# A gate table in DRAM: one-hot products replaced by indirect accumulating transfers, and 104 blocks spilled instead of 64

## The chip, the cores and the metric

One NeuronCore of one Trainium2 chip. TensorE is PE in the profile (its weight loads PEld), VectorE DVE, ScalarE ACT, GpSimd POOL, SyncE SP. SP issues the plain DMAs, POOL the indirect ones; both kinds run on the core's 16 DMA engines. The metric is the device time of one launch in microseconds (us), as the median of several runs.

## The reference, cut to what matters

One decoder layer on 512 tokens of width 1024: three kinds of attention beside each other, an output projection, then a retrieval network (PEER). Only the last is touched by the change:

```
qry = h @ w_q                                   # 8 heads x 256 per token
s1, s2 = scores of either half against 128 sub-keys
v1, i1 = top_k(s1, 16); v2, i2 = top_k(s2, 16)
top_s, pos = top_k(all v1[a] + v2[b], 16)       # of 256 pairs
expert = i1 * 128 + i2 at pos                   # 16 of 16384 experts per head
gate = softmax(top_s)
a = h . u[expert]; w = gelu(a) * gate
out = sum over the 128 (head, slot) of w * v[expert]
```

u and v are tables of 16384 rows of 1024 floats (64 MB each).

## The kernel before, in words

The tokens stand in four chunks of 128. After the attention (`attention`, L272) and the output projection (`mix_out`, L355) the retrieval is done in two ways.

Chunk 0 (`GC`) gathers its rows: for each of its 128 slots POOL gathers one u row per token by an indirect DMA (`gather`, L473), DVE multiplies it with the token's vector and sums (L482). When all 128 are there, the v rows are gathered too, scaled and added (L490 to L493), half of them on DVE, half by ACT and POOL.

Chunks 1 to 3 (`DC`, 384 tokens) go through the whole tables. The experts are cut into 128 blocks by their second index. For a block b, `u_parts` (L514) loads 512 KB of u and splits it into a high half (ACT) and a low half (DVE or POOL), and `a_block` (L521) forms gelu(u h) for 128 experts x 384 tokens with 24 PE matmuls of 384 columns. `w_block` (L628) multiplies this with the block's slice of a gate table (L645), which has a token's gate where it chose the expert and zero elsewhere, splits the product and a 512 KB block of v, and adds the product to eight accumulated sums in PSUM (18 PE matmuls of 512 columns, six banks). These banks are held to the end, so this second product starts only when the banks are free of other uses.

So the first `NSP` = 64 blocks are spilled: phase A (L603 to L610) forms their gelu(u h) and stores them in DRAM (`ad`), one step of the gathers after each block (`tc.issue_after` puts the step's instructions behind the last low split on that split's engine). The second stage (L655 on) forms the 64 others in place, loads the spilled ones again, and does the v products of all 128; what remains of the gathers goes beside it.

The queries, scores and top-16 of all heads are formed in a loop over four groups of two heads (L536 to L576): chunk 0's routing (`route`, L413: pair sums, top-16 of 50 candidates, look-up of the expert by compare, product and sum, L440 to L443, softmax of the gates) stands inside it, that of the other chunks after it. Then the gate table is made per chunk: expert and gate are transposed; for four tokens at a time DVE compares both indices with 0 to 127 (L591, L592), DVE or ACT multiplies the gate in (L595, L597), one PE product per token gives the 128 x 128 table of that token (L600), ACT copies it out (L601), and twelve stores of 2 MB put it into DRAM (L602). The second stage reads it back in 384 pieces of 64 KB (L637).

The order in which each engine issues its instructions is fixed when the program is built: a planner plays the program through with its own table of costs, and of what is ready takes what stands earlier in the program. Each engine then works its queue off in that order; POOL's holds its arithmetic and its indirect DMAs.

Of the kernel before, what the change touches and what calls it, by code (L numbers as in the profile page):

```python
# [22 lines left out]
P = 128  # L23
S = 512
NT = S // P
D = 1024
# [4 lines left out]
NK = 128  # L31
PH = 8
TK = 16
NSLOT = PH * TK
EPS = 1e-6
GC = 0
DC = [c for c in range(NT) if c != GC]
NSP = 64
GT = 32
LEAD = 2  # L40
NB = 4
BANKS = dict(s=4, t=2, o=2)
CYC = "stosstos"
WB = 4
SCB = 4
UL = "GGGG"
EM = 4
OGD = "AV"
GR = 1.0
TD = P * len(DC)  # L50
GROUPS = ((0, 1, 2), (3, 4, 5), (6, 7))
# [5 lines left out]
def layer_kernel(ctx, tc, x, xT, memT, mem, w_in, w_kv, w_out, w_q, cols, qk_gain, g_bc, subT, bias_tab,  # L57
# [4 lines left out]
    def tile_pool(**kw):  # L62
        return tc.tile_pool(reuse_waits="tile", **kw)
# [2 lines left out]
    dram = ctx.enter_context(tc.tile_pool(name="dram", bufs=1, space=DRAM))  # L66
    st = ctx.enter_context(tile_pool(name="st", bufs=8))
    xd = [dram.tile([P, D], F32, name=f"xd{c}") for c in range(NT)]
    gd = [[dram.tile([P, NK, GT], F32, name=f"gd{c}_{q}") for q in range(P // GT)] for c in range(len(DC))]
    ad = [dram.tile([P, TD], F32, name=f"ad{b}") for b in range(NSP)]  # L70

    ident = top.tile([P, P], F32, name="ident")
# [196 lines left out]
    tv = [[peer.tile([P, PH, TK], F32, name=f"tv{c}{i}") for i in range(2)] for c in range(NT)]  # L269
    ti = [[peer.tile([P, PH, TK], U32, name=f"ti{c}{i}") for i in range(2)] for c in range(NT)]  # L270

    def attention(chunks, yT, rg, name):  # L272
        base, W = chunks[0] * P, len(chunks) * P
        n_evac = 0
        last = chunks[-1]
        with tile_pool(name=f"sm{name}", bufs=2) as sm:
# [5 lines left out]
                              bias_tab[3 * i + 3:3 * i + 6, :, S - TW:S].rearrange("h p u -> p h u"))  # L282
            ones = sm.tile([P, P], F32, name="ones", bufs=1)
            V.memset(ones, 1.0)
            sqs = []
            for pair in range(8):
                o_ps = bank("o")
# [122 lines left out]
        for q in range(len(src)):  # L410
            V.max_index(idx[q][:, 8:16], vals[q][:, 8:16], rest[q])

    def route(c, dst=None, q0=0, nq=PH):  # L413
# [6 lines left out]
        V.tensor_scalar(tf[0], ti[c][0][:, qs, :], float(NK), None, ALU.mult)  # L420
        V.tensor_copy(tf[1], ti[c][1][:, qs, :])
        cv = tile_([nq, NCAND], "cv")
        ci = tile_([nq, NCAND], "ci")
        for d_, (one, two) in ((cv, [t[:, qs, :] for t in tv[c]]), (ci, tf)):
            off = 0
            for a, n in CAND:
                V.tensor_add(d_[:, :, off:off + n], two[:, :, 0:n], one[:, :, a:a + 1].to_broadcast([P, nq, n]))
                off += n
            V.tensor_add(d_[:, :, off:off + 8], one[:, :, 8:16], two[:, :, 0:1].to_broadcast([P, nq, 8]))
        wv = tile_([nq, TK], "wv")  # L430
        wi = tile_([nq, TK], "wi", U32)
        for q in range(0, nq, 4):
            some = range(q, min(q + 4, nq))
            top16(NCAND, [cv[:, r, :] for r in some], [wv[:, r, :] for r in some], [wi[:, r, :] for r in some], rp, "w")
        wf = tile_([nq, TK], "wf")
        V.tensor_copy(wf, wi)
        ex = tile_([nq, TK], "ex")
        for q in range(nq):
            eq = rp.tile([P, TK, NCAND], F32, tag="eq", name="eq", bufs=2)
            V.tensor_tensor(eq, wf[:, q, :, None].to_broadcast([P, TK, NCAND]),  # L440
                            iota[:, None, 0:NCAND].to_broadcast([P, TK, NCAND]), ALU.is_equal)
            (V if q < EM and nq == PH else G).tensor_mul(eq, eq, ci[:, q, None, :].to_broadcast([P, TK, NCAND]))
            V.tensor_reduce(ex[:, q, :], eq, AX.X, ALU.add)  # L443
        wm = tile_([nq], "wm")
        V.tensor_copy(wm, wv[:, :, 0])
# [7 lines left out]
        ef = ex.rearrange("p h k -> p (h k)")  # L453
        if c == GC:
            sl = slice(q0 * TK, (q0 + nq) * TK)
# [3 lines left out]
        gt = tile_([NSLOT], "gt")  # L459
        V.tensor_mul(gt.rearrange("p (h k) -> p h k", k=TK), pe, rb)  # L460
        ei = tile_([NSLOT], "ei", I32)
        V.tensor_copy(ei, ef)
        e12 = tile_([2, NSLOT], "e12", I32)
        V.tensor_scalar(e12[:, 0, :], ei, 7, None, ALU.arith_shift_right)
        V.tensor_scalar(e12[:, 1, :], ei, NK - 1, None, ALU.bitwise_and)
        f12 = tile_([2, NSLOT], "f12")
        V.tensor_copy(f12, e12)
        tp = quarters(bank("o"))[:, 0:3, :]
        for i, s_ in enumerate((f12[:, 0, :], f12[:, 1, :], gt)):
            T.transpose(tp[:, i, :], s_, ident)  # L470
        A.activation(dst, tp, AF.Copy)

    def gather(table, s_):  # L473
        row = gr.tile([P, D], F32, tag="row", name="row")
# [55 lines left out]
    with tile_pool(name="qa", bufs=1) as qa, tile_pool(name="qp", bufs=2) as qp:  # L530
        mix_out([GC] + DC, yT, rg, hT, "l")
        for t in ga:
            G.memset(t, 0.0)
        rp = ctx.enter_context(tile_pool(name="rp", bufs=1, side="right"))
        sub = qa.tile([P, 2 * PH, NK], F32, name="sub", bufs=1)
        for n in range(4):  # L536
            for k2 in range(KD // 2):
# [24 lines left out]
            for i in range(4):  # L562
# [8 lines left out]
                for j in range(len(DC)):  # L571
# [5 lines left out]
    with tile_pool(name="oh", bufs=2) as oh:  # L577
        loaded = 0
        steps = gather_all()
        for ci_, c in enumerate(DC):  # L580
            iT = oh.tile([P, 3, P], F32, tag="iT", name="iT")
            route(c, iT)
            for q in range(P // GT):
                stage = oh.tile([P, NK, GT], F32, tag="stage", name="stage")
                for t4 in range(0, GT, 4):
                    t0 = q * GT + t4
                    bc = lambda a: a[:, t0:t0 + 4, None].to_broadcast([P, 4, NK])
                    ib = iota[:, None, :].to_broadcast([P, 4, NK])
                    o1 = oh.tile([P, 4, NK], F32, tag="o1", name="o1", bufs=3)
                    o2 = oh.tile([P, 4, NK], F32, tag="o2", name="o2", bufs=3)  # L590
                    V.tensor_tensor(o1, bc(iT[:, 0, :]), ib, ALU.is_equal)  # L591
                    V.tensor_tensor(o2, bc(iT[:, 1, :]), ib, ALU.is_equal)  # L592
                    og = oh.tile([P, 4, NK], F32, tag="og", name="og", bufs=3)
                    if OGD[t4 // 4 % len(OGD)] == "V":
                        V.tensor_mul(og, o2, bc(iT[:, 2, :]))  # L595
                    for j in range(0 if OGD[t4 // 4 % len(OGD)] == "V" else 4):
                        A.activation(og[:, j, :], o2[:, j, :], AF.Copy, scale=iT[:, 2, t0 + j:t0 + j + 1])  # L597
                    gp = quarters(bank("s"))
                    for j in range(4):
                        T.matmul(gp[:, j, :], o1[:, j, :], og[:, j, :], start=True, stop=True)  # L600
                    A.activation(stage[:, :, t4:t4 + 4].rearrange("p e t -> p t e"), gp, AF.Copy)  # L601
                DMA.dma_start(gd[ci_][q], stage)  # L602
        for b in range(NSP):  # L603
            while loaded < min(b + 4, NSP):
                u_parts(loaded, loaded % 4, dict(G=G, V=V)[UL[loaded % len(UL)]])
                loaded += 1
            DMA.dma_start(ad[b], a_block(b))
            for s_ in range(int(GR * b), int(GR * (b + 1))):
                with tc.issue_after(last_lo[-1].ins):
                    next(steps)  # L610

    vs_src = v.rearrange("(a b) w -> b a w", b=NK)
    with tile_pool(name="vb", bufs=2) as vb:
# [14 lines left out]
        def w_block(n, b, ag):  # L628
# [2 lines left out]
                DMA.dma_start(ag, ad[b])  # L631
            g0 = b // NB * NB
            if g0 not in gtiles:
                gt = vb.tile([P, NB, len(DC), P], F32, tag="gt", name="gt")
                for ci_ in range(len(DC)):
                    for q in range(P // GT):
                        DMA.dma_start(gt[:, :, ci_, q * GT:(q + 1) * GT], gd[ci_][q][:, g0:g0 + NB, :])  # L637
# [7 lines left out]
            V.tensor_mul(w.rearrange("p (c t) -> p c t", t=P), ag.rearrange("p (c t) -> p c t", t=P),  # L645
                         gt[:, b % NB, :, :])
# [93 lines left out]
```

## Time and profile before

| | before |
|---|---|
| median of 3 runs | 1754.92 us (1753.0 to 1755.09) |
| span of the profiled execution | 1749.3 us; no time of its own stands beside it |
| PE busy | 1592.6 us (91%) |
| DVE busy | 1442.9 us (82%) |
| POOL busy | 968.3 us (55%) |
| ACT busy | 787.2 us (45%) |
| moved by DMA | 390.08 MB, mean 223 GB/s |
| mean granted clock of TensorE | 0.963 |

The span is from the first to the last instruction; the run's time is a little longer. Busy shares are averages over stages with different limits, so the rows below look at stretches. In a row of an instruction group, "idle" is the time in which the engine waited just before such an instruction, and for whom.

### The profile page before, as it was taken

The numbers are of one execution on the slowest core, as the hardware profiler recorded it, in microseconds if no ns is written. First come the engines' busy times: TensorE is split into PE (matmuls) and PEld (weight loads), VectorE is DVE, ScalarE is ACT, GpSimd is POOL, SyncE is SP. The second block draws the span as 40 slices with busy tenths as digits, with TensorE's granted clock in tenths as the row PEclk, the third lists the DMA queues.
The fourth block names the chain that finished last, engine by engine and source line by source line (L and its number), as shares of the span: only waits on it lengthen the run. The fifth ranks groups of instructions, "written<-read, shape, count | busy, mean of one in ns | idle before, by whom it ended". The sixth has DMA issues, their size and how long they took to land.

```text
span 1749.3 us, 23459 instructions
## 1 busy us (share of the span) xinstructions
PE 1592.6 (91%) x8045; PEld 1397.1 (80%) x8045; DVE 1442.9 (82%) x2552; ACT 787.2 (45%) x1287; POOL 968.3 (55%) x531
## 2 busy tenths in 40 slices
PE   7999989997686878878999999999999999899997
PEld 6886667997686777778998888888888888788885
DVE  6556745899999999979956877877889978889896
ACT  6345633332332555667843333334444443444442
POOL 4220013363776675734465544456778867788774
PEclk9999999998888989889999999999999999999998
DMA  8302034132566566557699999998999999898894
GB/s 322 106 25 103 1 121 144 49 125 90 181 212 198 182 218 216 176 222 280 231 315 325 279 318 288 315 286 279 291 287 278 317 290 275 255 309 276 288 277 171
DMA packets 317463, 390.08 MB, mean 223 GB/s; under 512 B 214944, under 2 KB 240544, under 8 KB 314656
## 3 DMA queue, kind: packets, MB, share of 16 engines
q1 hardware_dynamic: 280480, 254.36, 46.0%
q0 software_dynamic: 36864, 134.23, 21.6%
q8 instruction: 63, 1.03, 0.2%
q14 instruction: 56, 0.46, 0.1%
HBM read 346.57 MB, written 41.94 MB: 222 GB/s over the span
## 4 chain that ended last, share of the span: by engine, by line
PE 49%; DVE 36%; issue 5%; DMA 5%; ACT 2%; SPq 2%; POOL 2%; DVEq 0%; ACTq 0%; POOLq 0%
PE s L96 7%; PE s L97 7%; PE s L95 6%; PE t L95 5%; PE t L97 5%; PE t L96 5%; DVE row L482 5%; DVE o L591 5%; DVE o L592 4%; PE o L96 3%; PE o L97 3%; PE o L95 3%; DVE eq L440 2%; PE o L330 2%; DVE og L595 2%
## 5 line engine op out<-in xcount | busy, mean ns | idle before, releaser
L87 POOL TENSOR_TENSOR yT<-flat,yT 128x1024 fp32r<-128x1024 f32 x128 | 346.6, 2709 | 216.4 <-ACT yT L86 208.7
L95 PE MATMUL t<-hT,yT 128*128 128x384 f32 x1024 | 351.4, 343 | 26.1 <-ACT ag L527 26.1
L97 PE MATMUL t<-hT,yT 128*128 128x384 f32 x1024 | 351.4, 343 | 2.4 <-POOL yT L87 2.4
L96 PE MATMUL t<-hT,yT 128*128 128x384 f32 x1024 | 350.3, 342 | 0.0
L87 DVE TENSOR_TENSOR yT<-vr,yT 128x1024 fp32r<-128x1024 f32 x128 | 209.5, 1637 | 54.7 <-ACT yT L86 51.5
L475 POOL DMA_INDIRECT row<-u,exp_g x128 | 161.7, 1263 | 124.0 <-DVE row L482 88.3
L95 PEld LDWEIGHTS t<-hT,yT 128*128 128x128 f32 x1024 | 197.0, 192 | 32.5 <-ACT ag L527 27.3
L96 PE MATMUL s<-yT,ws 128*128 128x512 f32 x512 | 206.7, 405 | 11.1 <-DVE yT L87 10.8
L482 DVE SCALAR_TENSOR_TENSOR row<-row,hg 128x1024 f32<-128x1024 f32 x128 | 189.2, 1482 | 24.0 <-DMA row<-u,exp_g 24.0
L97 PE MATMUL s<-yT,ws 128*128 128x512 f32 x512 | 201.4, 402 | 4.2 <-DVE ws L87 4.2
L475 POOL DMA_INDIRECT row<-v,exp_g x128 | 156.1, 1219 | 84.9 <-DVE ga L493 49.6
L86 ACT ACTIVATE ws<-w 128x384 fp32r<-128x384 f32 x128 | 67.1, 524 | 299.4 <-DVE w L645 118.7
L97 PEld LDWEIGHTS t<-hT,yT 128*128 128x128 f32 x1024 | 196.8, 192 | 5.7 <-POOL yT L87 3.0
L96 PEld LDWEIGHTS t<-hT,yT 128*128 128x128 f32 x1024 | 196.8, 192 | 4.5
L86 ACT ACTIVATE yT<-flat 128x1024 fp32r<-128x1024 f32 x128 | 135.4, 1058 | 144.2 <-issue 53.6
L491 POOL TENSOR_TENSOR ga<-ga,row 128x1024 f32<-128x1024 f32 x64 | 164.1, 2564 | 26.1 <-ACT row L490 25.4
L95 PE MATMUL s<-yT,ws 128*128 128x512 f32 x512 | 165.1, 399 | 7.8 <-ACT ws L86 7.8
L86 ACT ACTIVATE yT<-vr 128x1024 fp32r<-128x1024 f32 x128 | 134.2, 1048 | 57.4 <-DMA vr<-v 44.0
L600 PE MATMUL s<-og,o 128*128 128x128 f32 x768 | 109.7, 296 | 54.8 <-DVE og L595 38.4
L600 PEld LDWEIGHTS s<-og,o 128*128 128x128 f32 x768 | 103.1, 208 | 63.4 <-issue 39.6
L87 DVE TENSOR_TENSOR ws<-w,ws 128x384 fp32r<-128x384 f32 x128 | 119.8, 937 | 41.0 <-ACT ws L86 36.2
L493 DVE SCALAR_TENSOR_TENSOR ga<-row,gw,ga 128x1024 f32<-128x1024 f32 x64 | 143.2, 2238 | 6.6 <-DMA row<-v,exp_g 6.4
(268 smaller groups left out, 3249.2 us busy)
## 6 DMA issues: line engine op xcount, KB each, us to landing
flat<-uT SPq DMA_DIRECT2D x128, 512.0 KB
vr<-v SPq DMA_DIRECT2D x128, 512.0 KB
gd<-stage SPq DMA_DIRECT2D x12, 2048.0 KB
gt<-gd SPq DMA_DIRECT2D x384, 64.0 KB
ad<-ag SPq DMA_DIRECT2D x64, 192.0 KB
agr<-ad SPq DMA_DIRECT2D x64, 192.0 KB
wraw<-w_in SPq DMA_DIRECT2D x8, 1024.0 KB
flat<-w_q SPq DMA_DIRECT2D x16, 512.0 KB
```

The lines of the kernel that those rows point to most:

```text
L86: A.activation(hi, src, AF.Copy)
L87: return (e_lo or V).tensor_sub(lo, src, hi.bitcast(F32))
L95: T.matmul(o, ah, bh, start=start, stop=False)
L96: T.matmul(o, ah, bl, start=False, stop=False)
L97: T.matmul(o, al, bh, start=False, stop=stop)
L475: G.indirect_dma_start(out=row, out_offset=None, in_=table, in_offset=bass.IndirectOffsetOnAxis(ap=exp_g[:, s_:s_ + 1], axis=0))
L482: V.scalar_tensor_tensor(row, row, 1.0, hg, ALU.mult, ALU.mult, accum_out=av[:, s_:s_ + 1])
L491: G.tensor_add(ga[1], ga[1], row)
L493: V.scalar_tensor_tensor(ga[0], row, gw[:, s_:s_ + 1], ga[0], ALU.mult, ALU.add)
L591: V.tensor_tensor(o1, bc(iT[:, 0, :]), ib, ALU.is_equal)
L592: V.tensor_tensor(o2, bc(iT[:, 1, :]), ib, ALU.is_equal)
L600: T.matmul(gp[:, j, :], o1[:, j, :], og[:, j, :], start=True, stop=True)
```

## The change

The table becomes one tensor in DRAM, `gd` of 128 blocks x 128 experts x 384 tokens (25.2 MB). During the attention it is filled with zeros from a zeroed tile, by six DMAs on SP's queue. The routing of chunks 1 to 3 moves into the query loop, four heads at a time (`RH`), after the second and the fourth group. It gives each slot the gate and the place in the table, and one indirect DMA per slot and chunk (3 x 128 = 384, issued by POOL) adds 128 gates of 4 bytes to 128 places. A head's transfers wait until those of the same chunk's previous head have landed, the first head's until the zeros have. The one-hots, their products, the copies and the twelve stores go. The table is read in 32 pieces of 768 KB, which wait for the last transfers.

Besides, 104 blocks instead of 64 are spilled, their low split of u is on DVE instead of POOL, and the expert look-up's product is on DVE for chunks 1 to 3 and on POOL for chunk 0 (before: four of eight heads of chunks 1 to 3 on DVE, all else on POOL).

```diff
-NSP = 64
+NSP = 104
...
+            zero = ga[1]
+            V.memset(zero, 0.0)
+            cells = gd.rearrange("b p t -> (b p t)").rearrange("(p r w) -> p r w", p=P, w=D)
+            for r in range(0, NK * TD // D, 8):
+                blank.append(DMA.dma_start(cells[:, r:r + 8, :], zero[:, None, :].to_broadcast([P, 8, D])).ins)
...
-            (V if q < EM and nq == PH else G).tensor_mul(eq, eq, ci[:, q, None, :].to_broadcast([P, TK, NCAND]))
+            (G if c == GC else V).tensor_mul(eq, eq, ci[:, q, None, :].to_broadcast([P, TK, NCAND]))
...
+        V.tensor_mul(gates[c][:, sl].rearrange("p (h k) -> p h k", k=TK), pe, rb)
+        V.tensor_scalar(places[c][:, sl], ef, float(TD), column[:, DC.index(c):DC.index(c) + 1], ALU.mult, ALU.add)
...
+    def scatter(c, h):
+        cells = gd.rearrange("b p t -> (b p t)")[:, None]
+        some = []
+        for s_ in range(h * TK, (h + 1) * TK):
+            ins = G.indirect_dma_start(
+                out=cells, out_offset=bass.IndirectOffsetOnAxis(ap=places[c][:, s_:s_ + 1], axis=0),
+                in_=gates[c][:, s_:s_ + 1], in_offset=None, compute_op=ALU.add).ins
...
+            after(ins, put[c, h - 1] if h else blank)
+            some.append(ins)
...
+        put[c, h] = some
...
+            if (n + 1) % (RH // 2) == 0:
+                heads = range(2 * (n + 1) - RH, 2 * (n + 1))
+                for c in DC:
+                    route(c, heads[0], RH)
+                for h in heads:
+                    for c in DC:
+                        scatter(c, h)
+    for b in range(NSP):
+        while loaded < min(b + 4, NSP):
+            u_parts(loaded, loaded % 4, V)
+            loaded += 1
+        DMA.dma_start(ad[b], a_block(b))
...
+                gt = vb.tile([P, NB, TD], F32, tag="gt", name="gt")
+                after(DMA.dma_start(gt, gd[g0:g0 + NB].rearrange("b p t -> p b t")).ins,
+                      [e for c in DC for e in put[c, PH - 1]])
```

## Rows read from the trace of the kernel before

**Rows 1.** Stretches: start and length, busy us of each engine, clock, DMA, GB/s.

```profile
core 0: us, PE busy (x) PEld busy (x) DVE busy (x) ACT busy (x) POOL busy (x), PEclk, DMA share, GB/s
0.00:40.00 40.00, 32.88 (x141) 26.76 (x141) 24.01 (x47) 27.62 (x49) 20.87 (x19) 1.00 0.91 329
136.00:243.00 107.00, 99.29 (x467) 65.78 (x466) 72.01 (x340) 63.59 (x193) 2.17 (x2) 0.98 0.17 62
315.00:905.00 590.00, 484.77 (x2889) 470.83 (x2888) 565.88 (x1411) 289.58 (x491) 346.36 (x166) 0.92 0.55 191
905.00:1200.00 295.00, 292.48 (x1396) 254.30 (x1396) 222.74 (x267) 104.79 (x143) 150.35 (x94) 1.00 0.96 307
905.00:1749.30 844.30, 813.42 (x3801) 698.51 (x3800) 691.29 (x585) 346.28 (x445) 554.32 (x315) 0.99 0.90 286
```

**Rows 2.** The page: the chain that ended last, share by engine.

```profile
PE 49%; DVE 36%; issue 5%; DMA 5%; ACT 2%; SPq 2%; POOL 2%; DVEq 0%; ACTq 0%; POOLq 0%
```

**Rows 3.** SP's queue in order of time, during the attention (start, length).

```profile
142.36 0.41 SPq L375 DMA_DIRECT2D ga<-g_bc  x1
229.24 0.33 SPq L541 DMA_DIRECT2D sub<-subT  x1
```

**Rows 4.** DVE's groups from 320 to 900 us: count, busy, mean, idle before.

```profile
L482 DVE SCALAR_TENSOR_TENSOR row<-row,hg 128x1024 f32<-128x1024 f32 x62 | 100.4, 1622 | 21.6 <-DMA row<-u,exp_g 21.6
L591 DVE TENSOR_TENSOR o<-iT,iota 128x512 f32<-128x512 f32 x96 | 96.7, 1022 | 0.0
L592 DVE TENSOR_TENSOR o<-iT,iota 128x512 f32<-128x512 f32 x96 | 89.5, 955 | 0.0
L440 DVE TENSOR_TENSOR eq<-wf,iota 128x800 f32<-128x800 f32 x32 | 41.7, 1320 | 0.0
L595 DVE TENSOR_TENSOR og<-o,iT 128x512 f32<-128x512 f32 x48 | 41.6, 868 | 0.0
```

**Rows 5.** PE's groups from 315 to 905 us.

```profile
L95 PE MATMUL t<-hT,yT 128*128 128x384 f32 x526 | 184.0, 350 | 26.1 <-ACT ag L527 26.1
...
L600 PE MATMUL s<-og,o 128*128 128x128 f32 x768 | 109.7, 296 | 54.8 <-DVE og L595 38.4 <-DVE o L591 15.1 <-ACT stage L601 1.2
```

**Rows 6.** Single lines of the code, whole span: duration in ns, min/median/max.

```profile
L482 DVE SCALAR_TENSOR_TENSOR row<-row,hg x128: 1194/1216/4674, 420.3 to 1185.5; 128x1024 f32<-128x1024 f32 x128
...
L440 DVE TENSOR_TENSOR eq<-wf,iota x32: 962/980/3178, 338.0 to 701.1; 128x800 f32<-128x800 f32 x32
...
L475 POOL DMA_INDIRECT row<-u,exp_g x128: 935/1230/1967, 412.9 to 1173.0; - x128
```

**Rows 7.** POOL's groups from 300 to 900 us.

```profile
L87 POOL TENSOR_TENSOR yT<-flat,yT 128x1024 fp32r<-128x1024 f32 x66 | 186.5, 2828 | 150.0 <-ACT yT L86 149.6
...
L442 POOL TENSOR_TENSOR eq<-eq,ci 128x800 f32<-128x800 f32 x20 | 45.5, 2283 | 51.8 <-DVE eq L440 50.4 <-PE s L600 1.3
L87 POOL TENSOR_TENSOR lo<-flat,hi 128x1024 fp32r<-128x1024 f32 x12 | 28.5, 2399 | 26.9 <-ACT hi L86 26.7 <-PE s L97 0.2
```

**Rows 8.** PE in order of time: the first and fourth of four matmuls.

```profile
999.77 0.33 PE L95 MATMUL t<-hT,yT 128*128 128x384 f32 x1
...
1000.29 0.34 PE L95 MATMUL t<-hT,yT 128*128 128x384 f32 x1
```

**Rows 9.** POOL in order of time: gathers issued back to back.

```profile
886.47 0.94 POOL L475 DMA_INDIRECT row<-u,exp_g  x1 [0.30 <-issue]
887.71 0.94 POOL L475 DMA_INDIRECT row<-u,exp_g  x1 [0.30 <-issue]
```

**Rows 10.** The page: DMA issues, count and KB each.

```profile
gt<-gd SPq DMA_DIRECT2D x384, 64.0 KB
```

**Rows 11.** DVE's weight products from 905 us on, by where the block comes from.

```profile
L645 DVE TENSOR_TENSOR w<-ag,gt 128x384 f32<-128x384 f32 x64 | 109.0, 1703 | 41.3 <-ACT ag L527 30.6 <-DMA gt<-gd 4.2 <-issue 3.6
...
L645 DVE TENSOR_TENSOR w<-agr,gt 128x384 f32<-128x384 f32 x64 | 44.6, 699 | 1.7 <-DMA flat<-uT 0.8
```

More of the change, by code (lines that the diff above doesn't have):

```diff
@@ L37 @@
 DC = [c for c in range(NT) if c != GC]
-NSP = 64
-GT = 32
+NSP = 104
 LEAD = 2
@@ L45 @@
 SCB = 4
-UL = "GGGG"
-EM = 4
-OGD = "AV"
+RH = 4
 GR = 1.0
@@ L68, in layer_kernel @@
     xd = [dram.tile([P, D], F32, name=f"xd{c}") for c in range(NT)]
-    gd = [[dram.tile([P, NK, GT], F32, name=f"gd{c}_{q}") for q in range(P // GT)] for c in range(len(DC))]
+    gd = dram.tile([NK, P, TD], F32, name="gd")
     ad = [dram.tile([P, TD], F32, name=f"ad{b}") for b in range(NSP)]
@@ L270, in layer_kernel @@
     ti = [[peer.tile([P, PH, TK], U32, name=f"ti{c}{i}") for i in range(2)] for c in range(NT)]
+    blank = []
     def attention(chunks, yT, rg, name):
@@ L411, in top16, with route @@
             V.max_index(idx[q][:, 8:16], vals[q][:, 8:16], rest[q])
-    def route(c, dst=None, q0=0, nq=PH):
+    def route(c, q0=0, nq=PH):
         qs = slice(q0, q0 + nq)
@@ L419, in route @@
         tf = [tile_([nq, TK], f"tf{i}") for i in range(2)]
-        V.tensor_scalar(tf[0], ti[c][0][:, qs, :], float(NK), None, ALU.mult)
-        V.tensor_copy(tf[1], ti[c][1][:, qs, :])
+        big = 0 if c == GC else 1
+        V.tensor_scalar(tf[big], ti[c][big][:, qs, :], float(NK), None, ALU.mult)
+        V.tensor_copy(tf[1 - big], ti[c][1 - big][:, qs, :])
         cv = tile_([nq, NCAND], "cv")
@@ L453, in route @@
         ef = ex.rearrange("p h k -> p (h k)")
+        sl = slice(q0 * TK, (q0 + nq) * TK)
         if c == GC:
-            sl = slice(q0 * TK, (q0 + nq) * TK)
             V.tensor_mul(gate_g[:, sl].rearrange("p (h k) -> p h k", k=TK), pe, rb)
@@ L458, in route, with after @@
             return
[L459 to L471, printed above, removed]
+        V.tensor_mul(gates[c][:, sl].rearrange("p (h k) -> p h k", k=TK), pe, rb)
+        V.tensor_scalar(places[c][:, sl], ef, float(TD), column[:, DC.index(c):DC.index(c) + 1], ALU.mult, ALU.add)
+    put = {}
+    def after(ins, earlier):
+        for e in earlier:
+            tc.add_manual_dep(ins, e.name, mybir.DependencyInfo(mybir.DependencyClass.Sync, mybir.DependencyReason.DATA))
+    def scatter(c, h):
[5 more added lines that the diff above has]
+                in_=gates[c][:, s_:s_ + 1], in_offset=None, compute_op=ALU.add).ins
+            if put or some:
+                tc.declare_no_dep(ins, group="put", reason="a head's experts differ, and so do chunks' tokens",
+                                  keep=put[c, h - 1] if h else [])
+            after(ins, put[c, h - 1] if h else blank)
+            some.append(ins)
+            tc.add_to_no_dep_group("put", ins)
+        put[c, h] = some
     def gather(table, s_):
@@ L534, in layer_kernel @@
         rp = ctx.enter_context(tile_pool(name="rp", bufs=1, side="right"))
+        gates = {c: rp.tile([P, NSLOT], F32, name=f"gates{c}") for c in DC}
+        places = {c: rp.tile([P, NSLOT], I32, name=f"places{c}") for c in DC}
+        column = rp.tile([P, len(DC)], F32, name="column")
+        G.iota(column, pattern=[[P, len(DC)]], base=0, channel_multiplier=1, allow_small_or_imprecise_dtypes=True)
         sub = qa.tile([P, 2 * PH, NK], F32, name="sub", bufs=1)
@@ L576, in layer_kernel @@
                       [ti[c][m % 2][:, m // 2, :] for c in DC], qp, "r")
[L577 to L610, printed above, removed]
@@ new lines, in layer_kernel @@
+            if (n + 1) % (RH // 2) == 0:
[5 more added lines that the diff above has]
+                        scatter(c, h)
+    loaded = 0
+    steps = gather_all()
+    for b in range(NSP):
[3 more added lines that the diff above has]
+        DMA.dma_start(ad[b], a_block(b))
+        for s_ in range(int(GR * b), int(GR * (b + 1))):
+            with tc.issue_after(last_lo[-1].ins):
+                next(steps)
@@ L633, in w_block @@
             if g0 not in gtiles:
[L634 to L637, printed above, removed]
+                gt = vb.tile([P, NB, TD], F32, tag="gt", name="gt")
+                after(DMA.dma_start(gt, gd[g0:g0 + NB].rearrange("b p t -> p b t")).ins,
+                      [e for c in DC for e in put[c, PH - 1]])
                 gtiles[g0] = gt
@@ L644, in w_block @@
             w = vb.tile([P, TD], F32, tag="w", name="w")
-            V.tensor_mul(w.rearrange("p (c t) -> p c t", t=P), ag.rearrange("p (c t) -> p c t", t=P),
-                         gt[:, b % NB, :, :])
+            V.tensor_mul(w, ag, gt[:, b % NB, :])
             ws = [vb.tile([P, TD], F32R, tag=f"ws{i}", name=f"ws{i}") for i in range(2)]
```

## The prediction

> **What bounds the kernel now.** I read the stages first (busy time of each engine per stretch), then DVE's and POOL's groups inside the middle stretch, then single instructions in order of time, and the chain last. From 315 to 905 us the routing, the one-hot table and the first spilled blocks run: DVE is busy 565.88 of 590 us, PE only 484.77 at a mean clock of 0.92, DMA a share of 0.55 [rows 1]. From 905 us to the end the second products run: PE is busy 813.42 of 844.30 us at clock 0.99, DMA 0.90 [rows 1]. So the middle belongs to DVE and the rest to PE, with DMA close behind. The chain agrees: 49% PE, 36% DVE [rows 2], DVE's lines being the one-hot compares and the row products. The profiled span is 1749.3 us; the median of the runs is 1754.92, so 5.6 us lie outside the span or between executions, and I add them at the end.
>
> **Zero fill.** It adds one DVE memset and six SP DMAs of 4.2 MB, 25.2 MB in all, in the attention stage. There SP issues nothing between 142.8 and 229.2 us [rows 3] and DMA runs at a share of 0.17 [rows 1]. At the 329 GB/s of the first 40 us [rows 1] the fill takes 77 us and ends near 225 us. The cover is that idle stretch. If writes ran at half that rate it would end near 297 us and hold up the loads that SP issues from 229 us on [rows 3], the output projection's weights among them, by up to 70 us; a gain is excluded, since nothing is taken away there. I take nothing: 77 us fits in 86.
>
> **What is removed from DVE, PE, ACT.** On DVE the compares and products of the one-hots: 96.7 + 89.5 + 41.6 = 228 us [rows 4]. On PE 768 passes, 109.7 us busy [rows 5]; on ACT the copies of both. Twelve 2 MB stores go too.
>
> **What is added to DVE.** The low halves of 104 u blocks move from POOL to DVE. A DVE instruction of the same class (two 128x1024 inputs) has a median of 1.216 us [rows 6]; 104 x 1.22 = 127 us, against 1.19 at the least and 1.62, the mean in this stretch [rows 4]: 124 to 168. The row products rise from 62 to at most 104: 42 x 1.3 = 55 us. Twelve products of the expert lookup come from POOL; the nearest row is their compare, 0.98 at best and 1.32 here [rows 4, 6]: 12 to 16, I take 14. Six routes on half-width tiles replace three, so the small instructions of a route, some 27 that don't shrink with the width, are issued three times more, 81 in all; at an estimated 0.12 us each (they have no row) 10 us.
>
> The row shows how two engines hinder each other: the row product takes 1.216 us at the median, 4.674 at most and 1.62 in this stretch [rows 4, 6], where POOL spends 186.5 us in 66 two-input subtractions [rows 7]. The Trainium skill ("SBUF — State Buffer", Who interferes with whom) says that a DVE instruction with two SBUF inputs contends with a GpSimd instruction that reads SBUF, and the holder keeps the shared port for its whole length. By that rule the excess goes with POOL's subtractions and the sum below is 25 us less (62 row products at 1.22 instead of 1.62), 844 instead of 870 us for DVE alone.
>
> I credit 11 us, on the 32 compares (1.32 to 0.98).
>
> Sum for DVE: 566 - 228 + 127 + 55 + 14 + 10 - 11 = 533 us, so DVE alone would let the stage end near 315 + 533/0.96 = 870 us.
>
> **The order inside the stage.** All the routing now stands in the query loop, ahead of the blocks in program order, and every split stands in DVE's queue beside it. Routing and top-16 are 566 - 228 - 100 = 238 us of DVE now (100 us being the row products [rows 4]) and 238 + 14 + 10 - 11 = 251 after, at 0.96 busy 261: from 315 to about 575 us. PE has its query products, 485 - 110 - 66 x 4.16 = 100 us; 4.16 is 24 matmuls at 0.173 us [rows 8], 66 blocks from the 526 first passes of eight [rows 5]. The rest of PE's time until 575 depends on how many u splits slip in. I take 20 blocks, which puts the end of routing at 600. Then 84 blocks x 4.16 = 349: phase A ends near **950 us**. Bounds: PE saturated from 300 us, 300 + 100 + 433 = 833; nothing slipping in, 575 + 433 = 1008. Where PE runs short its clock falls: 0.92 in this stretch now [rows 1].
>
> **The scatters.** 3 chunks x 128 slots = 384 accumulating DMAs on POOL, each of 128 elements. No row shows one. The nearest is the indirect gather, 128 descriptors too: back to back one each 1.24 us, 0.94 of it busy [rows 9]; the longest seen is 1.97 [rows 6], and 0.30 lies between. So 0.94 x 384 = 361 to 2.27 x 384 = 872 us; I take 1.24, 476 us. The first can go when the routes of heads 0 to 3 are through for the first chunk, about 420 us (half of the 261 us would be 445, with all three chunks); ahead of the last also stand four weight splits and four expert products, 19 us [rows 7]. The scatters end at 420 + 476 + 19 = 915 us if they go ahead of the gathers, at 1044 with all 104 gathers (129 us) between. Queued behind them on POOL are these gathers, the weight splits of the last quarter and the expert products. A head's scatters also wait for the same chunk's previous head, 32 scatters or 40 us earlier, so that wait costs nothing unless a landing takes that long. Every table load waits for the last landing; I take about 30 gathers in between and 950 us, level with phase A.
>
> **The second stage.** 40 of its u blocks go: 40 x 4.16 = 166, 844 - 166 = 678 us for PE. The 384 table loads of 64 KB [rows 10] become 32 of 768 KB. But the bytes are now crammed: v 67.1, table 25.2, spilled 104 x 0.197 = 20.4, u 24 x 0.524 = 12.6, 128 gathered rows of v 67.1, and the gathered rows of u that are left. With the 24 that the program leaves it is 205 MB, with 98 (30 done beside the scatters) 244. At the 307 GB/s of a stretch with DMA at 0.96 [rows 1] that is 668 and 795 us; at the 361 that 329 at a share of 0.91 stands for [rows 1], 568 and 676. The many short packets of the table go, so I take between, 345 GB/s: 244 / 345 = 707 us, DMA a little ahead of PE. DVE, 691.29 us busy in this stage now [rows 1], gets 34 more row products (98 for 64, 44 us) and is held up less by POOL's subtractions: the weight product takes 1.70 us beside a fresh block, 0.70 beside a spilled one [rows 11], 40 us over 40 blocks. At some 695 it is level too, and not ahead.
>
> **Sum:** 950 + 705 = 1655 of span, plus 5.6: **1660 us**.
>
> **Rivals.**
> *A, faster.* Gathers find room between scatters and PE is fed early: phase A ends near 880 (between 833 and 950), the second stage is PE's 678: 1564 us. For it: DVE's 533 us would allow 870. Against: the routes stand ahead of the splits.
> *B, the gain is lost to DMA.* 244 MB at 307 GB/s: 950 + 795 + 6 = 1751 us, no change. For it: DMA is already at 0.96 beside a saturated PE [rows 1]. Against: the table's 384 short loads [rows 10] leave the same queues.
> *C, slower.* The scatters cost more than a gather, in POOL's issue or because a 4-byte read-add-write holds POOL's DMA queue, and the second stage starts when the last has landed. Place: the wait of the first table load. With 678 us behind it the change breaks even at 1071 us, that is (1071 - 439) / 384 = 1.65 us per scatter if they go first, 1.31 with the gathers between. At 2.0 us: 439 + 768 + 678 + 6 = 1891. For it: POOL has gathers of 1.97 us [rows 6], and no accumulate is in the trace. Against: most gathers stay at 0.94 to 1.25 us [rows 6, 9].
>
> The Trainium skill ("DMA: Bandwidth & Descriptors", Anatomy of one DMA) puts a fixed cost of about 2.0 us on a DMA of this path, mostly the write receipt, longest to HBM. By it, paid one after the other, 384 x 2.0 would be rival C's 768 us; the gathers issued 1.24 us apart [rows 9] show that such latency overlaps, for gathers at least.
>
> **How the numbers follow.** Forecast 0.45 (1610 to 1710), A 0.20, B 0.10, C 0.22, and 0.03 that the parts cancel. A measurement here tells some 0.2% (3.5 us) from no change. Faster: 0.45 + 0.20 + 0.07 of B = 0.72; within 0.2%: 0.03 + 0.01 of B = 0.04; slower: 0.22 + 0.02 = 0.24. The range takes in A's 1564 with 14 us below it, B, and the start of C up to a scatter of 1.74 us: 1550 to 1790.
>
> **What would show it.** Right: DVE from 315 to 600 us full of routing, PE short of work there with a lowered clock; POOL an unbroken row of scatters about 1.24 us apart from 420 to past 900; the first table load waiting for the last landing near 950; then PE and DMA both over 0.9. Wrong: scatters over 1.6 us apart or waiting for landings (C); the first table load waiting on nothing and phase A's end set by DVE (A's side); the output projection late, beyond the 243 us at which its stage starts now (the fill not hidden).

## The result, and the profile after

The changed kernel takes 2025.65 us (median of 4 runs, 2023.37 to 2029.69) against 1753.96 us (4 runs, 1749.06 to 1755.09): a ratio of 1.1553, 95% interval 1.153 to 1.1577. It is slower, where 1660 us had been forecast; 272 us were lost where 95 were to be won. The profiled execution's span is 2021.5 us.

| stretch | forecast | measured |
|---|---|---|
| zero fill | hidden | hidden |
| first scatter | 420 us | 422.0 us |
| end of routing | 600 us | 932 us |
| 104 spilled blocks done | 950 us | 1091 us |
| one scatter, from start to start | 1.24 us | 1.86 us undisturbed, 2.00 in the mean |
| first table load | 950 us | 1239.2 us |
| from there to the end | 705 us | 782.3 us |

The busy time by stretch, which answers [rows 1]:

```profile
core 0: us, PE busy (x) PEld busy (x) DVE busy (x) ACT busy (x) POOL busy (x), PEclk, DMA share, GB/s
136.00:243.00 107.00, 97.54 (x459) 64.20 (x459) 72.52 (x341) 62.64 (x193) 2.17 (x2) 1.00 0.75 298
...
315.00:600.00 285.00, 182.99 (x1032) 177.27 (x1030) 207.61 (x1049) 77.60 (x113) 190.61 (x106) 0.83 0.40 95
600.00:1091.00 491.00, 357.98 (x1994) 355.35 (x1994) 166.72 (x215) 121.11 (x168) 408.04 (x242) 0.86 0.63 144
1091.00:1239.00 148.00, 0.01 (x1) 0.00 (x0) 0.22 (x1) 0.00 (x0) 123.60 (x80) 0.51 0.25 5
1239.00:1920.00 681.00, 650.01 (x2876) 533.00 (x2876) 600.51 (x646) 271.28 (x349) 437.39 (x273) 0.99 0.92 333
1920.00:2022.00 102.00, 0.00 (x0) 0.00 (x0) 46.63 (x22) 18.42 (x17) 75.24 (x49) 0.51 0.59 190
```

Three things are to be seen. From 315 to 1239 us no engine but POOL is near full (the 0.30 us between two scatters are not counted as busy), and from 1091 to 1239 us POOL works alone: that is no shared load, but one queue that everybody waits for. From 1239 to 1920 us TensorE is the bound again (650 of 681 us, clock 0.99). And 102 us follow in which TensorE has nothing left.

The scatters by their line (duration in ns, min/median/max, first and last start; then what the engine waited for just before them, and the time from issue to landing), and two of them in order of time:

```profile
L477 POOL DMA_INDIRECT gd<-gates,places x384: 1551/1554/4291, 422.0 to 1236.0; - x192
...
  issue: 117.7, 380
  DVE places L465: 38.1, 2
...
DMA to landing us min/median/max: 2.9/3.1/7.7
```

```profile
575.11 1.55 POOL L477 DMA_INDIRECT gd<-gates,places  x1 [0.30 <-issue]
576.97 1.55 POOL L477 DMA_INDIRECT gd<-gates,places  x1 [0.30 <-issue]
```

A gather had 0.94 us of POOL and 0.30 to the next [rows 9]; an adding scatter has 1.55 and 0.30. With the disturbed ones the page counts 650.5 us busy, and 117.7 us of issue: 768 us for 384, 2.00 us each. A landing takes 3.1 us while the next scatter starts 1.86 us after the last, so landings overlap and are not what paces them; nearly nothing waits for them.

Who waits for POOL (engine and line that wait, us in all, times, the longest):

```profile
PE t L94 <- DVE yT L84: 197.5, 5, 81.1
...
DVE ex L448 <- POOL eq L447: 183.1, 2, 92.5
...
DVE row L497 <- DMA row<-u,exp_g: 187.5, 11, 151.0
...
PE t L94 <- POOL yT L84: 154.0, 1, 154.0
```

Two expert products of chunk 0 stand behind a row of scatters on POOL; DVE's sums wait for them 183.1 us in two waits; the splits for TensorE stand behind these sums in DVE's queue, and TensorE waits for the splits. Later it is a row product that waits 151.0 us for a gather behind scatters, and TensorE waits 154.0 us for the first split that POOL makes for the second stage, also behind the last scatter:

```profile
1235.97 1.55 POOL L477 DMA_INDIRECT gd<-gates,places  x1 [0.30 <-issue]
1237.82 1.00 POOL L490 DMA_INDIRECT row<-u,exp_g  x1 [0.30 <-issue]
...
1239.21 0.92 SPq L637 DMA_DIRECT2D gt<-gd  x2
...
1242.25 6.11 DVE L497 SCALAR_TENSOR_TENSOR row<-row,hg 128x1024 f32<-128x1024 f32 x1 [151.04 <-DMA row<-u,exp_g]
1242.60 4.67 POOL L84 TENSOR_TENSOR yT<-flat,yT 128x1024 fp32r<-128x1024 f32 x2
```

The first table load starts 3.2 us after the last scatter's start. At the end the chain that ended last is no longer TensorE's [rows 2]:

```profile
DMA row<-v,exp_g 3%; DVE ga L508 1%; DMA vr<-v 1%; POOL row L490 1%; POOL ga L506 1%; DVE yT L84 0%; PE s L93 0%; PE s L94 0%; PE s L92 0%; DVE ws L84 0%; POOLq L736 0%; PE o L93 0%; PE o L94 0%; PE o L92 0%; DVE xr L675 0%
```

The shares add up to some 7% of the span only, so this chain tells of the end of the run and not of the whole: there it is gathers of v and the sums of them.

### The profile page after: what moved, and what is told of

Same layout as the page of the kernel before. It is cut to its first block, busy times and chain, and to the rows that moved or that the text cites. A ratio compares the mean times of both kernels' runs of the same rounds, so it can differ in the third digit from the quotient of the medians.

```text
span 2021.5 us, 21544 instructions
## 1 busy us (share of the span) xinstructions
PE 1484.2 (73%) x7268; PEld 1292.8 (64%) x7268; DVE 1209.5 (60%) x2501; ACT 639.8 (32%) x999; POOL 1302.6 (64%) x800
## 3 DMA queue, kind: packets, MB, share of 16 engines
q0 software_dynamic: 92160, 134.46, 26.3%
## 5 line engine op out<-in xcount | busy, mean ns | idle before, releaser
L477 POOL DMA_INDIRECT gd<-gates,places x384 | 650.5, 1694 | 156.5 <-issue 117.7
L94 PE MATMUL t<-hT,yT 128*128 128x384 f32 x1024 | 349.7, 342 | 351.5 <-DVE yT L84 197.5
L94 PEld LDWEIGHTS t<-hT,yT 128*128 128x128 f32 x1024 | 197.1, 192 | 354.6 <-DVE yT L84 199.1
L497 DVE SCALAR_TENSOR_TENSOR row<-row,hg 128x1024 f32<-128x1024 f32 x128 | 169.5, 1340 | 187.5 <-DMA row<-u,exp_g 187.5
L84 DVE TENSOR_TENSOR yT<-flat,yT 128x1024 fp32r<-128x1024 f32 x104 | 127.2, 1225 | 168.9 <-ACT yT L83 168.8
L490 POOL DMA_INDIRECT row<-v,exp_g x128 | 158.2, 1236 | 97.8 <-DVE ga L508 63.6
L93 PE MATMUL s<-yT,ws 128*128 128x512 f32 x512 | 205.0, 400 | 9.8 <-DVE yT L84 9.8
L94 PE MATMUL s<-yT,ws 128*128 128x512 f32 x512 | 202.6, 397 | 1.5 <-DVE ws L84 1.5
L84 DVE TENSOR_TENSOR yT<-vr,yT 128x1024 fp32r<-128x1024 f32 x128 | 170.7, 1336 | 24.5 <-ACT yT L83 24.4
L506 POOL TENSOR_TENSOR ga<-ga,row 128x1024 f32<-128x1024 f32 x64 | 158.2, 2471 | 23.6 <-ACT row L505 22.1
L92 PE MATMUL s<-yT,ws 128*128 128x512 f32 x512 | 147.7, 399 | 12.8 <-ACT yT L83 12.8
L84 DVE TENSOR_TENSOR ws<-w,ws 128x384 fp32r<-128x384 f32 x128 | 124.3, 971 | 52.8 <-ACT ws L83 51.8
L448 DVE TENSOR_REDUCE ex<-eq 128x16 f32<-128x800 f32 x32 | 30.7, 968 | 183.1 <-POOL eq L447 183.1
## 6 DMA issues: line engine op xcount, KB each, us to landing
gd<-ga SPq DMA_DIRECT2D x6, 4096.0 KB, 34.2
```

Source lines behind the costliest of these rows:

```text
L84: return (e_lo or V).tensor_sub(lo, src, hi.bitcast(F32))
L92: T.matmul(o, ah, bh, start=start, stop=False)
L93: T.matmul(o, ah, bl, start=False, stop=False)
L94: T.matmul(o, al, bh, start=False, stop=stop)
L477: ins = G.indirect_dma_start(out=cells, out_offset=bass.IndirectOffsetOnAxis(ap=places[c][:, s_:s_ + 1], axis=0), in_=gates[c][:, s_:s_ + ...
L490: G.indirect_dma_start(out=row, out_offset=None, in_=table, in_offset=bass.IndirectOffsetOnAxis(ap=exp_g[:, s_:s_ + 1], axis=0))
```

## The experiments

Each was run once beside the kernel before on the same chip (1740 to 1752 us there), but for the two that say otherwise. Theory: a scatter costs POOL's queue some 2 us, and what stands behind it waits. The rivals are named with each.

**1. No adding.**

```
-    in_=gates[c][:, s_:s_ + 1], in_offset=None, compute_op=ALU.add).ins
+    in_=gates[c][:, s_:s_ + 1], in_offset=None).ins
```

> The 384 scatters write their gates plainly, without adding; where two heads chose the same expert one gate is lost. Theory (POOL's price per scatter sets the start of the second stage), in two forms. If adding is what is dear: a scatter is 0.94 us busy at the median like a gather, 1.24 us from one to the next, the last one is issued near 422 + 19 + 476 + 30 = 950 us and the time is about 1700 us. If a scatter of 4-byte cells is dear with or without adding: median 1.55 us, last one near 1237 us, time 2015 to 2030 us. Rival (the queue's order, DVE waiting behind POOL, and not the price): time within 30 us of 2026 even if the median falls.

1816.04 us, more than expected. The scatters' line of this kernel, and their group on its page (busy time, mean, idle before):

```profile
L477 POOL DMA_INDIRECT gd<-gates,places x384: 965/969/4286, 426.1 to 1024.1; - x192
```

```profile
L477 POOL DMA_INDIRECT gd<-gates,places x384 | 434.3, 1131 | 156.2 <-issue 117.4
```

A plain scatter takes POOL 0.97 us at the median, as long as a gather; the adding costs 0.585 us more each. In the mean, with the disturbed ones, it is 434.3 + 117.4 = 552 us for 384, 1.44 us each. The first table load comes at 1026.5 instead of 1239.2 us, and the total falls by 210. Still, 1816 is slower than before, so the adding was not the only error. The page's row for POOL's DMA queue (packets, MB, share of 16 engines' span) for this kernel, for the changed one, and for the one without any scatter (experiment 3):

```profile
q0 software_dynamic: 49152, 134.46, 21.5%
```

```profile
q0 software_dynamic: 92160, 134.46, 26.3%
```

```profile
q0 software_dynamic: 36864, 134.23, 24.6%
```

384 plain scatters made 12,288 packets, 32 each, and 384 adding ones 55,296, 144 each.

**2. The other direction.** Gathers of the same 4-byte cells at the same places, in place of the scatters.

```
-    out=cells, out_offset=bass.IndirectOffsetOnAxis(ap=places[c][:, s_:s_ + 1], axis=0),
-    in_=gates[c][:, s_:s_ + 1], in_offset=None, compute_op=ALU.add).ins
+    out=gates[c][:, s_:s_ + 1], out_offset=None, in_=cells,
+    in_offset=bass.IndirectOffsetOnAxis(ap=places[c][:, s_:s_ + 1], axis=0)).ins
```

> Leaves out the filling of the table: each of the 384 scatters becomes an indirect gather of 128 four-byte cells of the same table at the same places (no write, no adding). Theory (it is the read-add-write that makes a scatter dear, not the four-byte size or the random place): about 0.95 us busy each and the total like that of the kernel without adding, 1790 to 1830 us. Rival (any indirect transfer of four bytes at scattered places takes 1.5 us): 1.5 us busy each and the total near 2000 us.

1801.33 us, and the line is

```profile
L477 POOL DMA_INDIRECT gates<-gd,places x384: 940/944/4293, 421.9 to 1012.2; - x192
```

Neither 4 bytes, nor scattered places, nor the direction is dear: 0.94 to 0.97 us in every case. Only the adding is.

**3. Half of the scatters, and none.**

```
-        for s_ in range(h * TK, (h + 1) * TK):
+        for s_ in range(h * TK, (h + 1) * TK, 2):
```

> Only every second slot is scattered: 192 scatters, half of the table's entries are left out. Theory: each costs POOL 1.86 to 2.0 us, so the last is issued near 422 + 19 + 192 x 2.0 + gathers = 840 to 900 us, then phase A sets the start of the second stage, near 1000 us; time 1700 to 1780 us. Rival (DVE's waits behind POOL): these halve, from 183 to about 90 us, and the time falls by about as much, to 1930 us.

> No scatter at all: the table stays zero, all else as in the changed kernel. Theory: nothing holds POOL's queue, phase A ends at 870 to 950 us and the second stage takes 680 to 710 us; time 1570 to 1660 us. Rival (the other parts of the change, 104 spilled blocks and the split on DVE, cost by themselves): time over 1755 us.

1768.70 us with 192 and 1597.55 us with none. The first table loads stand at (half first, then none)

```profile
L637 SPq DMA_DIRECT2D gt<-gd x32: 370/427/1305, 886.4 to 1713.0; - x32
```

```profile
L634 SPq DMA_DIRECT2D gt<-gd x32: 370/428/1377, 542.7 to 1541.5; - x32
```

The stores of the finished blocks end where the spilling ends (the changed kernel, half, none):

```profile
L609 SPq DMA_DIRECT2D ad<-ag x104: 319/326/433, 462.8 to 1090.4; - x104
```

```profile
L609 SPq DMA_DIRECT2D ad<-ag x104: 319/327/972, 462.7 to 1083.1; - x104
```

```profile
L606 SPq DMA_DIRECT2D ad<-ag x104: 319/327/485, 469.4 to 912.0; - x104
```

The second stage needs the blocks' end and the table. With none and with 192 scatters the table is there first (542.7 and 886.4 us), and the blocks set the start, at 912.0 and 1083.1 us; with 384 the table sets it, at 1239.2 us. From there to the end of the span it is 683.5, 683.8 and 782.3 us. So the 426 us of span between none and all have three parts. The first 192 scatters cost 171 us, though the last of them is issued long before the blocks' end: they hold the blocks up (TensorE waits 141.1 us for DVE's splits there, 16.7 without scatters). The next 192 put the last scatter from 883.2 to 1236.0 us, 1.84 us each, close to POOL's undisturbed price; the blocks' end hardly moves, so the start of the second stage moves by 156 us. The last 99 us are at the end of the second stage (experiment 7).

Without scatters the rest of the change is worth 143 us against the kernel before beside it (1740.45), so what is removed and added on DVE and TensorE is a gain by itself.

**4. Chunk 0's expert products on DVE**, so that DVE's sums don't wait behind scatters.

```
-            (G if c == GC else V).tensor_mul(eq, eq, ...
+            V.tensor_mul(eq, eq, ...
```

> The expert product of chunk 0 goes from POOL to DVE, so that DVE no longer waits behind scatters for it (183 us in two waits). Theory: POOL's scatters still stand one after the other from about 420 us; the last is issued some 35 to 60 us earlier (no gap between the two halves, no products on POOL), near 1190 us; time 1960 to 1990 us. Rival (DVE's waits are the cause): the whole 183 us come back, time about 1840 us.

2042.46 us; both expectations were missed. The wait for POOL's products is gone, and the same time stands at the row products:

```profile
DVE row L497 <- DMA row<-u,exp_g: 370.2, 9, 253.2
PE t L94 <- POOL yT L84: 241.3, 1, 241.3
```

The first table load came at 1224.1 us, 15 earlier. Taking away one wait behind the scatters lets DVE run up to the next one.

**5. All 128 blocks spilled**, to fill TensorE's idle stretch before the last landing.

```
-NSP = 104
+NSP = 128
```

> All 128 blocks spilled instead of 104. Theory (TensorE stands idle from 1091 us to the last scatter's landing at 1239, so 24 more blocks at 4.16 us, 100 us of TensorE, go in there free, but the end is that of the v gathers, which start when the u gathers are through): start of the second stage unchanged within 15 us, TensorE's last matmul 60 to 100 us earlier, the total 1930 to 2015 us. Rival (the second stage is bound by DMA, and more spilling adds bytes to it): 2020 to 2050 us.

2033.69 us: missed by the theory (TensorE's last product is at 1931 us, 12 later instead of 60 to 100 earlier), and the rival's number came for another reason. A block's product is made in three passes over split halves. Third passes (L94, eight per block) up to the first table load (this kernel to 1250 us, then the changed one to 1239):

```profile
L94 PE MATMUL t<-hT,yT 128*128 128x384 f32 x864 | 294.4, 341 | 206.3 <-DVE yT L84 206.2
```

```profile
L94 PE MATMUL t<-hT,yT 128*128 128x384 f32 x832 | 284.2, 342 | 197.5 <-DVE yT L84 197.5
```

108 blocks against 104: TensorE did not want for blocks, it was kept from them. DVE waited 149.1 us for one row there too.

**6. The gathers not woven between the blocks**, with all 128 spilled.

```
-NSP = 104
+NSP = 128
-GR = 1.0
+GR = 0.0
```

> All 128 blocks spilled, and the gathers of u rows are not woven into the blocks but stand behind them all. Theory (TensorE's idle 150 us before the last scatter lands are DVE's: a row product waits at the head of its queue for a gather that stands behind scatters on POOL, and the splits for TensorE stand behind that row product): TensorE gets through all 128 first products, 1024 first passes against 864, before the first table load, which comes 20 to 45 us earlier (1205 to 1230) as 22 gathers go from ahead of it; its last matmul is near 1800 us. What that gives to the whole is lost again to a longer tail of gathers, 256 of them after the last scatter instead of 234: 1990 to 2080 us. Rival (TensorE is idle there for want of POOL's splits or of the transfers of uT): again about 110 of the 128 before the first table load.

1999.88 us, inside the range. Up to the first table load TensorE now makes 992 recorded third passes, 124 blocks, and stands idle after that (second row):

```profile
1091.00:1182.00 91.00, 91.00 (x527) 91.00 (x526) 25.74 (x21) 31.66 (x44) 77.59 (x45) 1.00 0.70 165
1182.00:1323.00 141.00, 6.07 (x36) 5.75 (x34) 0.00 (x0) 0.00 (x0) 117.87 (x77) 0.53 0.23 0
```

These are 16 blocks more than in experiment 5, with the row products behind more of the blocks: that holds for the row products as the hindrance. The wait itself stays. TensorE stands idle about as long, and DVE waits as long for one row (experiment 5 from 905 to 1260 us, then this run from 1205 us on):

```profile
DVE row L497 <- DMA row<-u,exp_g: 175.0, 3, 149.1
```

```profile
DVE row L497 <- DMA row<-u,exp_g: 156.9, 6, 149.2
```

The date of the first table load was missed (1323.7, not 1205 to 1230). The planner put 35 gathers of u ahead of the first scatter, which starts at 489.3 instead of 422.0 us, and 25 between that and the load: 60 in all, where the changed kernel has 23. So this run moved more than one thing, and the total is not to be read for one of them. TensorE's stretch from the first table load to its last product is 612 us here (to 1935), against 680.

**7. No gathers of v** but four.

```
+            if s_ >= 4:
+                return
             row = gather(v, s_)
```

> Leaves out the gathers of v rows but four, with their products and sums (chunk 0's output is incomplete); scatters as they are. Theory (TensorE's last matmul is at 1919 us whatever the gathers do, and the last 100 us are their tail alone): the stretch after the last scatter falls from 782 to 650 to 690 us, the total to 1900 to 1935 us. Rival (the gathers' 67 MB and their DVE work also hold TensorE up in the second stage, or DMA is its bound): the total falls by 150 us or more, under 1875 us.

1913.79 us. The last matmul ends at 1906.4 us, where it was at 1919.1, and the span 5.3 us behind it, at 1911.7. So the last 102 us of the changed kernel are the gathers' tail. Beside TensorE's products the gathers of v cost at most another 24 us: from the first table load to the last matmul it is 656 us here (from 1250.3) and 680 with them.

**8. Parts of the change alone, in the kernel before.**

```
-NSP = 64
+NSP = 104
```

> The kernel before with 104 blocks spilled instead of 64, nothing else. Theory (the spilling alone moves 40 x 4.16 = 166 us of TensorE from the second stage to the middle one and is worth nothing without the one-hots' removal): 1720 to 1775 us, so that the 150 us between the kernel before and the one without a scatter are the one-hot products'. Rival (the spilling is itself a gain, as it fills TensorE while DVE bounds the middle): under 1700 us.

```
-UL = "GGGG"
+UL = "VVVV"
```

> The kernel before with the low halves of its spilled u blocks on DVE instead of POOL, nothing else. Theory (DVE bounds the middle stretch; 66 splits x 1.22 = 80 us come to it, 36 us go since POOL's subtractions no longer slow its row products and compares): 44 us slower, 1780 to 1810 us. Rival (the splits on DVE are done twice as fast as on POOL and TensorE waits less for them): not slower than 1755 us.

1781.13 us with 104 blocks spilled, 30 us slower than before and a little over the expected range, and 1776.33 us with the splits on DVE, 26 us slower than before where 44 had been worked out. Both cost time by themselves; so the 143 us of experiment 3 need the one-hot work to go. What else changed with it (the routing in the query loop, the table loads of 768 KB) was not run alone.

**9. A mix that should beat both:** one chunk scattered (128 scatters), two by one-hot products, 64 blocks spilled. First with the scatters in the query loop:

```
+SD = DC[:1]
+OD = DC[1:]
-            (n + 1) % (RH // 2) == 0: route and scatter each c in DC
+            (n + 1) % (RH // 2) == 0: route and scatter each c in SD
+        one-hot tables for each c in OD, as in the kernel before
+UL = "GVGV"
```

> A mix of the two kernels: one of the three chunks is scattered (128 scatters, during the query loop), the other two go by one-hot products as before, 64 blocks spilled, their splits in turn on POOL and DVE. Theory (a scatter costs 1.9 us of POOL's queue and nothing else, and POOL had some 240 us idle between 315 and 905 us, while DVE bounds that stretch and loses a third of its one-hot work, 76 us): 1670 to 1730 us. Rival (POOL becomes the bound of the stretch, 346 us as before and 240 of scatters, which can start only at 420 us): 1760 to 1830 us.

1816.91 us: the rival's. The stretch in which the scatters run (this kernel from 450 to 750 us, in two halves; then TensorE's longest wait there):

```profile
450.00:600.00 150.00, 72.93 (x314) 69.41 (x313) 96.76 (x416) 28.20 (x37) 129.78 (x79) 0.71 0.48 108
600.00:750.00 150.00, 76.48 (x430) 74.47 (x431) 78.97 (x111) 43.75 (x79) 131.91 (x77) 0.75 0.47 114
```

```profile
PE t L101 <- POOL yT L91: 128.1, 7, 27.7
```

POOL's total was not too much (it is busy for 88 of the next 155 us); the order fits better: u splits and expert products stand between rows of 16 scatters, some 30 us each. So the next two kernels put the scatters one ahead of each one-hot group and one after each block, with the splits on DVE, or every fourth on POOL:

```
+                    next(puts)
                     V.tensor_tensor(o1, bc(iT[:, 0, :]), ib, ALU.is_equal)
...
             DMA.dma_start(ad[b], a_block(b))
+            next(puts, None)
-UL = "GVGV"
+UL = "VVVV"   (the second one: "VVVG")
```

> The mix again (one chunk scattered, two by one-hot products, 64 blocks spilled), but the scatters stand one at a time behind the routing, one ahead of each one-hot group and one after each spilled block, so that nothing waits behind a long row of them on POOL; the u splits are all on DVE. Theory (a scatter costs 1.9 us of POOL's queue and nothing else): DVE in the middle stretch has 566 - 76 (a third of the one-hot work) + 80 (66 splits at 1.22) - 31 (row products and compares no longer slowed by POOL's subtractions) = 539 us, 27 less than before: 1700 to 1740 us. Rival (POOL's queue of 243 us of scatters still delays gathers or the first table load): 1760 us or more.

> As the kernel with the spread scatters, but every fourth u split stays on POOL (2.7 us each there). Theory: DVE is relieved of 16 x 1.22 = 20 us, POOL's queue gets 43 us in the block loop, where it then has 1.24 + 1.9 + 0.7 = 3.8 us per block of 4.2: within 15 us of the one with all on DVE, 1690 to 1740 us. Rival: a split that waits behind a scatter and a gather holds TensorE up, 1750 us or more.

Both were timed in three rounds: 1795.37 us, ratio 1.0249 (1.0203 to 1.0296), and 1803.05 us, ratio 1.0309 (1.0262 to 1.0356). Both are faster than the first mix and slower than the kernel before. But the scatters were not spread: in the traces they stand in rows of up to 16 again, as the planner ordered them, so one at a time is not tested. The gathers stand between these rows, and DVE's row products wait for them: of the waits from 600 to 905 us, first in the mix with all splits on DVE, then in the kernel before,

```profile
DVE row L520 <- DMA row<-u,exp_g: 98.2, 8, 21.1
```

```profile
DVE row L482 <- DMA row<-u,exp_g: 24.0, 5, 10.3
```

That is 74 us more, and the last store of one-hot tables comes at 954.7 instead of 880.6 us. The splits on DVE alone (experiment 8) put it at 932.7 us and cost 26 us, so the two causes are not separated here. No version was found that beats the kernel before and has the whole table.

## Why the prediction was wrong

**Right, with their numbers.** The zero fill: six stores landing in 34.2 us each at the median, DMA at 0.75 from 136 to 243 us instead of 0.17, and TensorE busy 97.5 us there instead of 99.3 [rows 1]: nothing held up. The first scatter (422). The splits on DVE: 104 at a mean of 1.225 us, where 1.22 was taken. TensorE in the second stage: 680 us from the first table load to its last product, where 678 was worked out. And that the removal is a gain: without scatters the kernel takes 1597.55 us.

DVE's contention went as told. The row products from 315 to 1239 us in the changed kernel:

```profile
L497 DVE SCALAR_TENSOR_TENSOR row<-row,hg 128x1024 f32<-128x1024 f32 x22 | 26.5, 1213 | 33.7 <-DMA row<-u,exp_g 33.7
```

1213 ns in the mean, where POOL has only 12 subtractions and 8 products left, against 1622 [rows 4] beside 66 subtractions [rows 7]. By the rule of the Trainium skill ("SBUF — State Buffer", Who interferes with whom), that a DVE instruction with two SBUF inputs and a GpSimd one that reads SBUF shut each other out, this was to be expected, and the trace agrees. The second run of experiment 8 moves little but these subtractions (59 of the 66) and shows it too (315 to 905 us, before, then that run):

```profile
L482 DVE SCALAR_TENSOR_TENSOR row<-row,hg 128x1024 f32<-128x1024 f32 x65 | 104.0, 1604 | 24.0 <-DMA row<-u,exp_g 24.0
```

```profile
L482 DVE SCALAR_TENSOR_TENSOR row<-row,hg 128x1024 f32<-128x1024 f32 x120 | 158.2, 1319 | 6.4 <-DMA row<-u,exp_g 6.3
```

In the changed kernel it bought nothing, since DVE no longer bounded the stretch. The 0.12 us for a small instruction of a route had no row behind it and was low: the changed kernel's additions of 8 columns (L432) take 0.148 us in the mean.

**The step that failed: "The nearest is the indirect gather ... I take 1.24, 476 us."** It measured 1.86 us undisturbed and 2.00 in the mean, 768 us, which is 292 more than the 476; the first table load came 289 us later than forecast. Two things were missing in the 1.24. One is the adding, a property that was not in the trace of before: without it the row of scatters takes 552 us, 216 less. The other, 76 us, is that a mean was needed and the undisturbed value was taken: a plain scatter, too, takes 1.44 us in the mean, and experiment 1's first table load is 76 us late. The bounds, 0.94 to 2.27, did hold the price, but the value taken stood at the row nearest in form, and the sum had a break-even of 1.65 us in between. Rival C's own sum for 2.0 us was 1891. The rest up to 2025 is 32 us of gathers, products and waits between the scatters and 104 us of the second stage (782 instead of C's 678).

The Trainium skill ("DMA: Bandwidth & Descriptors", Anatomy of one DMA) puts descriptor generation at "small, variable" and most of a DMA's fixed cost into the write receipt. For the pace of a long row of them that is no guide here: the 3.1 us to landing overlap, and the 1.55 us on POOL, which do not, set it. The measurement decides.

**A cover that was not there.** The prediction named what is queued behind the scatters on POOL ("gathers, the weight splits of the last quarter and the expert products") and charged 19 us of POOL for it. It did not follow the wait further: the expert products on POOL feed DVE's sums, and the u splits stand behind these in DVE's queue. So "the end of routing at 600" became 932 us (the last destination is written then), and TensorE reached 104 blocks at 1091 us instead of 950. In the changed kernel this delay is hidden, since the last scatter comes another 148 us later. What it costs where it is not hidden, experiment 3 shows: 171 us with half of the scatters. The 192 scatters of the first half of the heads stand nearly in one row, from 422 to 813 us, and 160 of the second half from 924 to 1236 us, long against everything that shares the queue.

**The second stage, 705 forecast, 782 measured.** The 707 was DMA's, 244 MB at 345 GB/s; DMA was no bound (0.92, and TensorE reached its 680 beside it). What was mis-sized is the gathers. Only 22 row products were done by the first table load, not 30, and then 106 u rows and 128 v rows go through four buffers one after the other: 234 in 782 us, 3.3 us each, 102 us longer than TensorE needs. What sets the 3.3 us was not tested. DVE's load was told as level at 695 us; that the gathers are a chain of their own, with an end of their own, was not.

Of the signs that I had named for "wrong", the first came in full: scatters over 1.6 us apart, with the first table load behind the last. The clock fell where TensorE stood idle (0.83 to 0.86 up to 1091 us and 0.51, the level of 1.2 GHz, while it had nothing to do); in this account that is a consequence.

## What to carry to other kernels

When a change puts many transfers on an engine that also computes, price one such transfer by a run with exactly its options, since an option that the trace of before doesn't have (here the adding) can cost more than the rest of the issue. Then follow the queue two steps on: what stands behind the transfers, who waits for that, and what stands behind the waiter in its own queue; the engine's total idle time does not tell it. And ask of a stage that loses its bound which chain of small transfers will end last there.

## What the runs showed of the hardware

- An indirect transfer of 128 elements costs POOL 0.94 to 0.97 us at the median, whether it gathers rows of 4 KB (undisturbed), gathers single cells or scatters them, and 0.30 us lie between two. With adding it costs 1.55 us.
- It can take longer. From 422 to 530 us, where DVE is busy for 100 of 108 us, 48 adding scatters took POOL 91.5 us, 1.91 each; from 1091 to 1237 us, with DVE idle, 79 took 122.1 us, 1.55 each. DMA was busier in the first stretch, too (0.63 against 0.25), so which of them does it is not shown.
- The packets differ with the adding: 144 for an adding scatter, 32 for a plain one (differences of the pages' queue rows). But they do not set the price on POOL: the kernel without scatters makes 36,864 packets for its 256 gathers of 4 KB rows, also 144 each, and such a gather takes 0.94 us.
- By the page's shares, the 55,296 packets of the adding scatters took 26.3% of 16 x 2021.5 us less 24.6% of 16 x 1595.5 us, 8506 - 6280 = 2226 us of one engine, an estimated 40 ns each (if the gathers' packets took the same in both runs). Spread over 16 engines that is 139 us, and it did not set the pace, which was POOL's.
